# Row sums, output-weight sums and the first output chunk's sums moved from GpSimd to VectorE, in a hybrid attention and retention layer

## The chip, the cores and the metric

One core of a Trainium2 chip. The metric is device time in microseconds (us) for one execution. The engines are written as the profile writes them: PE (TensorE), DVE (VectorE), ACT (ScalarE), POOL (GpSimd), SP (SyncE, which here only issues DMAs). Each engine works through its own queue in order, and semaphores tie the queues together.

## The reference

One layer over 2048 rows of width 1024: RMSNorm, one input projection to 7168 columns, two branches (chunk-banded attention and chunkwise retention, 8 heads each), a gated merge, an output projection with the residual, and a final RMSNorm. What matters here is the end of it:

```python
branch_a = einsum('bsf,fd->bsd', o_a * silu(g_a), w_out_attn[l])      # 512 -> 1024
o_r = retention_chunkwise(qr, kr, v_r, gn_gain[l])                    # per-head group norm inside
branch_r = einsum('bsf,fd->bsd', o_r * silu(g_r), w_out_ret[l])       # 1024 -> 1024
mixed = sigmoid(m_a) * branch_a + sigmoid(m_r) * branch_r
x = x + einsum('bsd,de->bse', mixed, w_out[l])
return rms_norm(x, final_gain)
```

All of it is float32.

## The kernel before, in words

**Split products.** Each float32 operand is split in a high part (ACT casts it to the PE's rounded float32 type) and a lower part (a subtraction, on DVE or POOL), and a product of two operands is three matmuls: high by high, high by low, low by high. A product over 512 rows of depth is 4 x 3 = 12 matmuls of 128x128 by 512 columns. One step of the kernel is three matmuls; a product is four steps.

**Strassen.** The two large projections and the output projection use a seven-product scheme. For each chunk of 256 columns or rows there are quarters `b11` to `b22` of the streamed operand and four sums `t1` to `t4` of them (`sum`, three of them chained), and the resident operand `R[0]` to `R[6]` holds quarters and sums of the other side, each as high and lower parts. The seven products go into PSUM banks named `x`, `y`, `v`, `z`, `w` and are gathered on DVE into `u2`, `u3`, `c22`.

**Stages near the change.** Behind attention and retention of the second half of the rows come
- `ba0`, `ba1`: attention's output projection, 4 chunks each, plain products `ps_ba`; each result is gated on DVE (`ga`) and stored as `ta` to DRAM (`tas`);
- `br0`, `br1`: retention's output projection, 4 chunks of 8 products each, `ps_br`. The chunk's weights `raw_br` are loaded, cast by ACT (`wh_br`) and their lower parts made on DVE (`wl_br`). Two products end one group: DVE computes `gr = (gr + 1) * psum` (line 1287), POOL adds the stored `ta` to it (line 1288), and SP stores the sum to `mxs`. The loads of `gr` and `ta` use a ring of six tiles and are issued by SP, in program order with all other SP loads and stores;
- beside these, `finish_yr` makes the resident operand of `br`: SP loads `yr`, `yv`, `rb`; DVE multiplies `yr` by the gain and gate (line 1242), POOL by the row scale `rb` (line 1245), ACT casts (line 1251), DVE subtracts (line 1252). 24 such rows in this stage;
- during `br1`, `fill_wo` is called four times: it loads four quarters of the output weights (`wo`) and makes three sums of them (`ws`) on DVE and POOL, and the high and lower parts of `R[0]`, `R[1]`, `R[3]`. `place_wo` then fills `R[4]`, `R[5]`, `R[2]`, `R[6]` while the last chunk of `br1` releases them;
- `out`: eight chunks of seven products, streamed from `mxs` by ACT's queue (`raw_out`). The first chunk goes through its products in the order (0, 4, 3, 1, 2, 5, 6), so into `x`, `z`, `x`, `y`, `v`, `w`, `z`. Its sums come from POOL; the lower parts for products 2 and 5 (of `t3` and `t4`) also, all others from DVE. Each result is added to the residual rows `xr`, squared on ACT, and multiplied by the final gain `fg` on POOL.

**What sets the order.** PE and SP always run in program order. ACT, DVE and POOL do so too while `strict` is on. It is off from the end of retention until product 2 of the last `br1` chunk (in the trace around 1752 us); there a scheduler orders these three queues by its own costs. From then on the code's order holds: `later(n, fn)` puts work `n` steps ahead, and what falls due is emitted between two steps of PE. The second use of bank `x` in output chunk 0 needs `u2` (a copy by ACT, `u_out` in the trace) to have read the first.

Of the kernel before, what the change touches and what calls it, by code (L numbers as in the profile page):

```python
# [16 lines left out]
ALU = mybir.AluOpType  # L17
# [56 lines left out]
def hybrid_kernel(  # L74
# [30 lines left out]
    def r32(ap):  # L105
        return ap.bitcast(F32)
# [7 lines left out]
    def E(name, dt=F32, shape=(P, 512)):  # L114
        return epool[0].tile(list(shape), dt, tag="e", name=name)
# [33 lines left out]
    class Sometimes(Ordered):  # L149
# [3 lines left out]
    pe, act, dve, pool = Ordered(nc.tensor), Sometimes(nc.scalar), Sometimes(nc.vector), Sometimes(nc.gpsimd)  # L153
# [12 lines left out]
    R = [  # L166
        [res.tile([P, 4, B], F32R, tag=f"r{m}{n}", name=f"r{m}{n}") for n in range(2)]
        for m in range(7)
    ]
# [75 lines left out]
    def later(n, fn):  # L245

        order[0] += 1
        deferred.append((steps[0] + n, order[0], fn, free[0]))
        deferred.sort(key=lambda e: e[:2])
# [8 lines left out]
    def put(lag, dst, src):  # L258

        later(lag, lambda: dma(dst, src))  # L260
# [75 lines left out]
    class Strassen(Chunk):  # L336
# [5 lines left out]
        def sum(self, dst, one, two, ring=None):  # L342
            b = self.b
            if dst in b:
                return
            name = f"{dst}_{self.job.name}_{self.c}"
            t = wp.tile([P, 4, P], F32, tag="t", bufs=SUMS, name=name) if ring is None else \
                ring(name).rearrange("p (k c) -> p k c", k=4)
            b[dst] = self.shaped(t)
            pool.tensor_tensor(b[dst], b[one], b[two], ALU.subtract)  # L350

        def before(self):

# [16 lines left out]
        def prepare(self, n):  # L370
            self.sums(n)
            for s in SUMS_OF:
                if s[0] == PRODUCTS[n][1]:
                    self.sum(*s)
            late = pool if n in self.job.lo_pool else dve
            self.make(n, self.b[PRODUCTS[n][1]], late)

        def product(self, n):
# [855 lines left out]
    def finish_yr(h, b, m, lead, hold=0):  # L1234

        a, u, r = (E(f"{n}_{h}_{b}") for n in ("yr", "yv", "rb"))
        dma(a, orscr[h // 2][b][h % 2])
        dma(u, urscr[h][b])
        dma(r, rsscr[b // 2][8 * b + h].rearrange("(o d) -> o d", o=1).broadcast_to([P, B]))

        def gated():
            dve.scalar_tensor_tensor(a, a, gn[:, h:h + 1], u, ALU.mult, ALU.mult)

        later(lead, gated)
        later(lead + 2, lambda: pool.tensor_tensor(a, a, r, ALU.mult))
        if m is None:
            put(lead + 8, yrscr[h], a)
            return
        wh, wl = (w[:, h % 4, :] for w in R[m])
        at = max(lead + 5, hold - steps[0])  # L1250
        later(at, lambda: act.copy(wh, a))
        later(at + 2, lambda: dve.tensor_tensor(wl, a, r32(wh), ALU.subtract))
# [31 lines left out]
    def ep_br(s):  # L1284
        def epilogue(c, i, j, ps, got):
            g, ta = got
            dve.scalar_tensor_tensor(g, g, 1.0, ps, ALU.add, ALU.mult)
            pool.tensor_tensor(g, g, ta, ALU.add)
            put(7, mxscr[2 * s + i][2 * c + j], g)

        return epilogue

    wo = {}

    def fill_wo(k):

        a = {}
        for i, j in ((0, 0), (1, 0), (1, 1), (0, 1)):
            a[i, j] = E(f"wo_{i}_{j}_{k}")
            row = (4 * j + k) * P  # L1300
            dma(a[i, j], w_out[0, row:row + P, 512 * i:512 * i + 512])
        s2, s3, s4 = (E(f"ws{n}_{k}") for n in (2, 3, 4))
        wo[4, k], wo[5, k], wo[2, k], wo[6, k] = s2, s3, a[1, 1], s4

        def place(m, t, eng):
            later(1, lambda: act.copy(R[m][0][:, k, :], t))
            later(3, lambda: eng.tensor_tensor(R[m][1][:, k, :], t, r32(R[m][0][:, k, :]), ALU.subtract))

        def sums():
            dve.tensor_tensor(s3, a[1, 0], a[0, 0], ALU.subtract)  # L1310
            place(0, a[0, 0], pool)
            dve.tensor_tensor(s2, s3, a[1, 1], ALU.add)

        def rest():
            pool.tensor_tensor(s4, a[0, 1], s2, ALU.subtract)
            place(1, a[0, 1], dve)
            pool.tensor_tensor(a[1, 0], a[1, 0], a[1, 1], ALU.add)
            place(3, a[1, 0], dve)

        later(10, sums)  # L1320
        later(13, rest)

    def place_wo(m, first, every):
        for k in range(4):
            def low(k=k):
                eng = pool if k == 2 else dve
                eng.tensor_tensor(R[m][1][:, k, :], wo[m, k], r32(R[m][0][:, k, :]), ALU.subtract)

            later(first + every * k, lambda k=k: act.copy(R[m][0][:, k, :], wo[m, k]))
            later(first + every * k + 2, low)  # L1330
# [623 lines left out]
    for h in range(HEADS):  # L1954
        later(10 + 44 * h, lambda h=h: finish_yr(h, 0, None, 18))
# [12 lines left out]
    for s, (first, every, of) in enumerate((YR_0, YR_1)):  # L1968
        for n, (i, h) in enumerate((i, h) for i in range(1 - s, 2) for h in range(HEADS)):
            hold = free_at + h % 4 if s and i and h > 3 else 0  # L1970
            later(
                first + every * n // of,
                lambda s=s, i=i, h=h, hold=hold: finish_yr(h, 2 * s + i, RYR[s][i, h // 4], 8, hold),
            )
# [60 lines left out]
```

## Time and profile before

| | us |
|---|---|
| median of 3 runs | 1936.4 |
| lowest and highest run | 1934.06, 1937.48 |
| the profiled execution | 1934.51 |
| its span (first to last instruction) | 1932.7 |
| PE busy | 1877.7 (97%) |
| DVE busy | 1353.5 (70%), 2530 instructions |
| ACT busy | 931.1 (48%) |
| POOL busy | 885.1 (46%), 733 instructions |

The TensorE clock granted was 0.997 of full speed over the span. A row of the timeline gives start, duration, engine, line, operation, output and inputs, shapes, count, and in brackets how long the engine had been idle and what released it. A row of waits gives who waited, for whom, total us, times, the longest. In a group of instructions the figures are: total busy us, mean ns, idle us before them and the releasers. L143 is the line of a helper through which all operations in strict order pass, so there one goes by tiles. The merge runs from about 1495 us, `br0` from 1586, `br1` from about 1673, the output projection from 1765 to the end.

### The profile page before, as it was taken

To read this page: it belongs to the slowest core of one execution; us is meant where nothing else is said; L and a number is where in the kernel's file an instruction comes from. 1 tells how busy PE (TensorE), PEld (TensorE's weight loads), DVE (VectorE), ACT (ScalarE), POOL (GpSimd) and SP (SyncE) were. 2 spreads that over 40 slices of the span, in tenths; PEclk is the share of its full clock that TensorE was granted. 3 is DMA by queue.
4 is the path that set the end of the run, shared out by engine and by line. 5 is a ranking of instruction groups with operands and counts; after the bars stand their busy time and mean duration, and the time that the engine had idled before them with its cause. 6 is when DMAs were issued, how large, how long until landed. Compare 5 with 4: busy or idle time off the path is not lost. (4 is left out here: it accounts for less than half of the span.)

```text
span 1932.7 us, 31908 instructions
## 1 busy us (share of the span) xinstructions
PE 1877.7 (97%) x10437; PEld 1614.5 (84%) x10437; DVE 1353.5 (70%) x2530; ACT 931.1 (48%) x1931; POOL 885.1 (46%) x733
## 2 busy tenths in 40 slices
PE   7999999999999999999999999999999999998998
PEld 6899889888888887899889888888888878886886
DVE  6979788677756558879797777775555654557665
ACT  7555554666655545343333556664555221223554
POOL 0313515546546664223515444544564115547775
PEclk9999999999999999999999999999999999999999
DMA  6586876565659988675666555555998999976673
GB/s 196 165 269 204 264 262 223 182 192 171 173 158 282 272 243 286 197 252 186 206 236 216 161 162 175 161 157 161 290 269 270 323 345 328 325 262 222 208 236 132
DMA packets 325557, 435.93 MB, mean 226 GB/s; under 512 B 29880, under 2 KB 191184, under 8 KB 325392
## 3 DMA queue, kind: packets, MB, share of 16 engines
q1 hardware_dynamic: 260096, 368.35, 59.6%
q10 hardware_dynamic: 65296, 65.55, 11.1%
q8 instruction: 83, 1.36, 0.3%
q14 instruction: 82, 0.67, 0.1%
HBM read 288.14 MB, written 145.64 MB: 224 GB/s over the span
## 5 line engine op out<-in xcount | busy, mean ns | idle before, releaser
L143 POOL TENSOR_SCALAR pr<-pr,rsum 128x640 f32<-128x640 f32 (+4 forms) x128 | 96.1, 751 | 213.7 <-DVE ptl L143 104.8
L143 PE MATMUL ps_g_z<-r,wh_g 128*128 128x512 f32 x448 | 143.7, 402 | 2.7 <-DVE c_g L143 2.7
L143 PE MATMUL ps_g_x<-r,wh_g 128*128 128x512 f32 x448 | 143.2, 401 | 1.2 <-ACT u_g L143 1.1
L143 DVE CUSTOM_DVE_ANT_0 pr<-wide,bt 128x640 f32<-128x640 f32 (+4 forms) x128 | 94.3, 736 | 62.4 <-PE wide L143 55.6
L143 ACT ACTIVATE pr<-pr,mn 128x640 f32<-128x640 f32 (+4 forms) x128 | 98.0, 766 | 81.4 <-DVE mn L143 81.4
L143 DVE TENSOR_TENSOR ptl<-tp,pth 128x384 fp32r<-128x384 f32 x168 | 96.1, 573 | 41.3 <-ACT pth L143 37.4
L143 ACT CAST pth<-tp 128x384 fp32r<-128x384 f32 x168 | 84.5, 515 | 68.5 <-PE tp L143 65.6
L143 POOL TENSOR_TENSOR l_vr<-vrt,h_vr 128x512 fp32r<-128x512 f32 x32 | 47.2, 1476 | 117.0 <-ACT h_vr L143 69.3
L143 POOL TENSOR_TENSOR sl<-sm,sh 128x384 fp32r<-128x384 f32 x64 | 70.4, 1099 | 58.3 <-ACT sh L143 46.3
L143 PEld LDWEIGHTS tp<-ident,pr 128*128 128x128 f32 x560 | 71.2, 140 | 27.3 <-POOL pr L143 2.8
L143 PE MATMUL po<-pth,va 128*128 128x256 f32 x336 | 92.5, 296 | 1.2 <-DMA va<-vas 0.7
L143 POOL TENSOR_TENSOR wl_g<-t_g,wh_g 128x512 fp32r<-128x512 f32 x56 | 75.0, 1339 | 39.9 <-ACT wh_g L143 33.2
L143 PE MATMUL tp<-ident,pr 128*128 128x128 f32 x560 | 89.1, 272 | 3.0 <-POOL pr L143 1.9
L143 ACT CAST wh_p<-raw_p 128x512 fp32r<-128x512 f32 x111 | 68.0, 619 | 49.9 <-PE ps_p_y L143 15.5
L143 DVE TENSOR_TENSOR wl_p<-raw_p,wh_p 128x512 fp32r<-128x512 f32 x111 | 86.2, 783 | 7.4 <-ACT wh_p L143 6.9
L143 DVE TENSOR_TENSOR sm<-sr,dm 128x384 f32<-128x384 f32 x64 | 35.6, 556 | 78.5 <-DMA dm<-in_dmask_dram 28.2
L143 PE MATMUL wide<-ka,qa 128*128 128x384 f32 (+1 forms) x448 | 88.3, 313 | 2.2 <-DVE mn L143 2.1
L143 PEld LDWEIGHTS wide<-ka,qa 128*128 128x128 f32 x448 | 74.6, 188 | 18.6 <-DVE mn L143 8.7
L143 PE MATMUL po<-ptl,va 128*128 128x256 f32 x336 | 88.3, 284 | 1.4 <-DVE ptl L143 0.2
L143 PE MATMUL ps_g_x<-r,wl_g 128*128 128x512 f32 x224 | 88.2, 394 | 0.0
L143 PE MATMUL ps_g_z<-r,wl_g 128*128 128x512 f32 x224 | 88.1, 393 | 0.0
L143 PEld LDWEIGHTS ps_g_x<-r,wh_g 128*128 128x128 f32 x448 | 75.8, 189 | 10.7 <-ACT u_g L143 2.5
(930 smaller groups left out, 6217.3 us busy)
## 6 DMA issues: line engine op xcount, KB each, us to landing
raw_g<-in_w_in_dram ACTq DMA_DIRECT2D x56, 512.0 KB, 5.1
raw_p<-in_w_in_dram ACTq DMA_DIRECT2D x50, 512.0 KB, 5.7
qa<-qas SPq DMA_DIRECT2D x128, 128.0 KB, 3.1
qr<-qrs SPq DMA_DIRECT2D x128, 128.0 KB, 4.6
vr<-vrs SPq DMA_DIRECT2D x64, 256.0 KB, 5.4
ka<-kas SPq DMA_DIRECT2D x56, 256.0 KB, 3.2
va<-vas SPq DMA_DIRECT2D x40, 256.0 KB, 3.3
kds<-kdt_k SPq DMA_DIRECT2D x32, 256.0 KB, 3.3
```

The costliest lines, as they stand in the source:

```text
L143: return tc.keep_in_program_order(op(*a, **k))
```

## The change

Where an instruction ran on POOL, it runs on DVE: the product with `rb` in `finish_yr` (only the 24 calls in the merge, `m` not None), the row sum in `ep_br` (32), two sums and a lower part in each `fill_wo` (12), one lower part in each `place_wo` (4), and in output chunk 0 the four sums and the two lower parts that were on POOL (6; `lean()` is true there only). Nothing else moves; the later output chunks keep their sums and those lower parts on POOL.

```diff
             b[dst] = self.shaped(t)
-            pool.tensor_tensor(b[dst], b[one], b[two], ALU.subtract)
+            (dve if self.lean() else pool).tensor_tensor(b[dst], b[one], b[two], ALU.subtract)
+
+        def lean(self):
+            return self.job.name == "out" and self.c == 0
...
-            late = pool if n in self.job.lo_pool else dve
+            late = pool if n in self.job.lo_pool and not self.lean() else dve
...
-        later(lead + 2, lambda: pool.tensor_tensor(a, a, r, ALU.mult))
+        later(lead + 2, lambda: (pool if m is None else dve).tensor_tensor(a, a, r, ALU.mult))
...
             dve.scalar_tensor_tensor(g, g, 1.0, ps, ALU.add, ALU.mult)
-            pool.tensor_tensor(g, g, ta, ALU.add)
+            dve.tensor_tensor(g, g, ta, ALU.add)
             put(7, mxscr[2 * s + i][2 * c + j], g)
...
-            place(0, a[0, 0], pool)
+            place(0, a[0, 0])
...
-            pool.tensor_tensor(s4, a[0, 1], s2, ALU.subtract)
-            place(1, a[0, 1], dve)
-            pool.tensor_tensor(a[1, 0], a[1, 0], a[1, 1], ALU.add)
-            place(3, a[1, 0], dve)
+            dve.tensor_tensor(s4, a[0, 1], s2, ALU.subtract)
+            place(1, a[0, 1])
+            dve.tensor_tensor(a[1, 0], a[1, 0], a[1, 1], ALU.add)
+            place(3, a[1, 0])
...
-                eng = pool if k == 2 else dve
-                eng.tensor_tensor(R[m][1][:, k, :], wo[m, k], r32(R[m][0][:, k, :]), ALU.subtract)
+                dve.tensor_tensor(R[m][1][:, k, :], wo[m, k], r32(R[m][0][:, k, :]), ALU.subtract)
```

More of the change, by code (lines that the diff above doesn't have):

```diff
@@ L1303, in fill_wo, with place @@
         wo[4, k], wo[5, k], wo[2, k], wo[6, k] = s2, s3, a[1, 1], s4
-        def place(m, t, eng):
+        def place(m, t):
             later(1, lambda: act.copy(R[m][0][:, k, :], t))
-            later(3, lambda: eng.tensor_tensor(R[m][1][:, k, :], t, r32(R[m][0][:, k, :]), ALU.subtract))
+            later(3, lambda: dve.tensor_tensor(R[m][1][:, k, :], t, r32(R[m][0][:, k, :]), ALU.subtract))
         def sums():
             dve.tensor_tensor(s3, a[1, 0], a[0, 0], ALU.subtract)
-            place(0, a[0, 0], pool)
+            place(0, a[0, 0])
             dve.tensor_tensor(s2, s3, a[1, 1], ALU.add)
         def rest():
-            pool.tensor_tensor(s4, a[0, 1], s2, ALU.subtract)
-            place(1, a[0, 1], dve)
-            pool.tensor_tensor(a[1, 0], a[1, 0], a[1, 1], ALU.add)
-            place(3, a[1, 0], dve)
+            dve.tensor_tensor(s4, a[0, 1], s2, ALU.subtract)
+            place(1, a[0, 1])
+            dve.tensor_tensor(a[1, 0], a[1, 0], a[1, 1], ALU.add)
+            place(3, a[1, 0])
         later(10, sums)
```

## The prediction

> **What bounds the kernel now.** I began with the page: how busy each engine is and the chain that ended last.
>
> ```profile
> span 1932.7 us, 31908 instructions
> PE 1877.7 (97%) x10437; PEld 1614.5 (84%) x10437; DVE 1353.5 (70%) x2530; ACT 931.1 (48%) x1931; POOL 885.1 (46%) x733
> PE 7%; DVE 0%; ACT 0%; issue 0%; DVEq 0%
> 1787.88 3.00 PE ps_out_z L143 x12
> 1790.88 2.72 PE ps_out_x L143 x12
> ```
>
> TensorE (PE) is busy 97% of the span. The chain in order of time (the last two rows) shows 2.72 us for one product of twelve matmuls, and from 1787.88 on it runs product after product with no wait between them until the last one; the tail behind that is not touched. So the change can only win, or lose, PE's waits before that point. These are PE's waits from the merge to the second output chunk:
>
> ```profile
> PE ps_out_x L143 <- ACT u_out L143: 2.8, 1, 2.8
> PE ps_br_(0, 0)_20577 L143 <- DVE wl_br_(0, 1)_20526 L300: 2.2, 1, 2.2
> PE ps_out_y L143 <- DVE wl_out L143: 1.1, 1, 1.1
> PE ps_out_z L143 <- DVE c_out L143: 0.7, 1, 0.7
> PE ps_ba_(0, 0)_19020 L143 <- ACT wh_ba_(0, 0)_18940 L299: 0.7, 1, 0.7
> PE ps_out_w L143 <- POOL wl_out L143: 0.5, 1, 0.5
> ```
>
> Five lie between 1744 and 1788: 2.2 in the last chunk of `br1`, then 2.8, 1.1, 0.5 and 0.7 in output chunk 0, together 7.3 us. That is the pot. The `ba` wait (0.7) hangs on a late weight load, which is not edited. Next I read the vector queues around the two large waits.
>
> ```profile
> 1743.13 1.29 POOL L1307 TENSOR_TENSOR r<-wo,r 128x512 fp32r<-128x512 f32 x1 [11.34 <-ACT r L1306]
> 1744.38 1.71 POOL L1288 TENSOR_TENSOR gr<-gr,ta 128x512 f32<-128x512 f32 x1
> 1743.17 1.80 DVE L1310 TENSOR_TENSOR ws<-wo,wo 128x512 f32<-128x512 f32 x1 [2.78 <-DMA wo<-in_w_out_dram]
> 1744.89 1.74 DVE L300 TENSOR_TENSOR wl_br_(0, 1)_20526<-raw_br,wh_br_(0, 1)_20525 128x512 fp32r<-128x512 f32 x1
> 1746.56 1.77 DVE L1312 TENSOR_TENSOR ws<-ws,wo 128x512 f32<-128x512 f32 x1
> 1750.78 0.67 DVE L1287 SCALAR_TENSOR_TENSOR gr<-gr,ps_br_(1, 0)_20493 128x512 f32<-128x512 f32 x1
> 1771.96 0.68 DVE L143 SCALAR_TENSOR_TENSOR gr<-gr,ps_br_(1, 1)_20702 128x512 f32<-128x512 f32 x1
> 1772.56 0.68 DVE L143 TENSOR_TENSOR wl_out<-raw_out,wh_out 128x512 fp32r<-128x512 f32 x1
> 1773.16 1.76 DVE L143 TENSOR_TENSOR r<-wo,r 128x512 fp32r<-128x512 f32 x1
> ```
>
> The same 128x512 subtraction on VectorE (DVE) takes 0.68 us with starts 0.60 us apart when GpSimd (POOL) is idle (1772.56), and 1.74 to 1.80 when POOL runs beside it (1743.17, 1744.89, 1773.16). POOL needs 1.29 alone and 1.71 contended. The product with a PSUM operand is 0.67 to 0.68 either way. So a pair side by side costs each engine about 1.75 us for what DVE alone does in 0.60 each. The Trainium skill (SBUF — State Buffer, section Who interferes with whom) says that a VectorE instruction with two SBUF inputs and a GpSimd instruction that reads SBUF exclude each other for a whole instruction; 0.68 against 1.74 agrees.
>
> The 2.2 us wait is this: `wl_br_(0, 1)` was queued behind the weight difference at 1743.17, and both were stretched. The 2.8 us wait comes by a longer way, through SyncE (SP) and ScalarE (ACT):
>
> ```profile
> SPq L143 <- POOL gr L1288: 8.5, 2, 4.6
> 1746.11 0.32 SPq L143 DMA_DIRECT2D mxs<-gr  x1
> 1753.23 0.32 SPq L143 DMA_DIRECT2D mxs<-gr  x1
> 1756.58 0.32 SPq L143 DMA_DIRECT2D ta<-tas  x1
> 1759.68 1.29 POOL L143 TENSOR_TENSOR gr<-gr,ta 128x512 f32<-128x512 f32 x1 [2.29 <-DMA ta<-tas]
> 1763.95 0.32 SPq L143 DMA_DIRECT2D ta<-tas  x1
> 1764.80 0.42 SPq L143 DMA_DIRECT2D xr<-in_x_dram  x1
> 1769.10 0.37 ACTq L143 DMA_DIRECT2D raw_out<-mxs  x1
> 1769.56 0.62 ACT L143 CAST wh_out<-raw_out 128x512 fp32r<-128x512 f32 x1 [3.63 <-DMA xr<-in_x_dram]
> 1773.21 0.57 ACT L143 COPY u_out<-ps_out_x 128x512 f32<-128x512 f32 x1
> ```
>
> SP issues in order and stood up to 4.6 us for one row sum `gr += ta` on POOL (1753.23). Each later `ta` load comes 3.35 us behind the store of a row sum whose buffer it takes (1753.23 to 1756.58; it landed 3.1 us on, when the sum at 1759.68 began), and the stores queue behind it, so a late sum makes the whole row of `ta`, store, `ta`, store late, up to the `xr` load at 1764.80. By the profile ACT's load of `raw_out` (1769.10) was released by that `xr` landing, and seven casts behind the one at 1769.56 stands `u_out`, which ends at 1773.8 (1773.21 + 0.57) and for which PE waits. So what starts the row is a sum on POOL, and each link behind it is a store and a load.
>
> **The change part by part.** 78 instructions go from POOL to DVE: 24 products `yr`, 32 sums `gr += ta`, 12 in `fill_wo`, 4 in `place_wo`, 4 sums and 2 lower parts of output chunk 0. The groups:
>
> ```profile
> L1288 POOL TENSOR_TENSOR gr<-gr,ta 128x512 f32<-128x512 f32 x29 | 44.4, 1538 | 55.7 <-DVE gr L1287 34.6 <-issue 11.4 <-DMA rb<-rss 4.2
> L1245 POOL TENSOR_TENSOR yr<-yr,rb 128x512 f32<-128x512 f32 x24 | 31.7, 1320 | 77.4 <-DVE yr L1242 35.8 <-DMA ga<-mas 24.4 <-DMA rb<-rss 17.3
> L1252 DVE TENSOR_TENSOR r<-yr,r 128x512 fp32r<-128x512 f32 x24 | 17.9, 745 | 57.2 <-ACT r L1251 57.2
> L1310 DVE TENSOR_TENSOR ws<-wo,wo 128x512 f32<-128x512 f32 x4 | 5.7, 1434 | 17.5 <-DMA wo<-in_w_out_dram 17.5
> L143 POOL TENSOR_TENSOR gr<-gr,ta 128x512 f32<-128x512 f32 x3 | 4.7, 1562 | 4.7 <-DMA ta<-tas 2.3 <-DVE gr L143 1.2 <-DVE r L143 1.2
> 1580.00:1740.00 160.00, 160.00 (x707) 132.49 (x706) 81.56 (x106) 32.00 (x55) 73.81 (x51) 1.00 0.90 308
> 1740.00:1790.00 50.00, 42.69 (x183) 33.77 (x182) 38.82 (x39) 19.07 (x37) 38.09 (x25) 1.00 0.66 219
> ```
>
> (The last two rows are busy time by stretch: its length, then PE, PEld, DVE, ACT and POOL. PE's 42.69 of 50.00 is the pot again.) DVE takes 78 x 0.60 = 47 us, POOL gives up some 110 (78 x about 1.4).
>
> *The 24 `yr` products.* DVE now idles 57.2 us over the 24 lower parts, 2.4 each, waiting for ACT behind POOL's 1.32. With the product on DVE (0.60) that chain is shorter by about 0.7, and the product fills idle time. New risk: DVE itself now waits for `rb`. POOL's three waits for it total 17.3 us, but mostly count POOL's idleness before DVE was ready. Bounds: no cost, to DVE held for a few us. PE is busy all 160.00 us from 1580 to 1740, although DVE stood most of its 17.5 us of waits for `wo` in there; waits of a few us are covered. I take 0.
>
> *The 32 row sums.* 0.60 each on DVE, directly behind the product that feeds them. What is queued behind a sum that waits for `ta`: lower parts and PSUM evacuations. In the trace one sum of 32 waited for `ta` (2.3 in the row of three; the row of 29 names none), and that one because the store two rows above it was late. With the product at 1750.78 followed at once by its sum, the store goes out at 1752.1 at the latest, not 1753.23.
>
> *Output weights (16).* In `fill_wo` a row of four weights costs DVE 7 instructions in place of 4. In the last row: the difference at 1743.17 takes 0.60, `wl_br_(0, 1)` the next 0.60, so it ends at 1744.4; PE, which waited 2.2 us until 1746.6 (1744.89 + 1.74), wants it at 1744.4. If the scheduler puts the newly moved lower part ahead, 0.6 us of the wait stays. Gain of this wait by itself 1.6 to 2.2. Then come two sums, the difference, two lower parts and the product of 1750.78: 8 instructions by 0.60 behind 1743.17, and about 0.7 for the casts, put it at 1748.7, its sum at 1749.3, the store at 1750.0: 3.2 us earlier. The sum at 1744.38 no longer waits behind a lower part (its store was at 1746.11), so SP is freed some 3 to 4 us earlier too, and loads ahead of it move up: I take the SP row as 3.2 to 5.5 earlier, 4.4 in the middle.
>
> *Output chunk 0 (6).* Here the order is the written one. Count DVE's queue from the end of PE's last product but two of `br1` (half 1, column 0 of the last chunk): first that half's `gr` product, its sum, and then lower parts of weights, two sums of the chunk and so on; the last `gr` product is the 14th, its sum the 15th, the lower part for the next product into `ps_out_x` the 16th, for `ps_out_y` the 20th, for `ps_out_v` the 24th. At 0.60 they are there after 9.6, 12.0 and 14.4 us. PE wants them after 4, 5 and 6 products of 2.72: 10.9, 13.6 and 16.3. So DVE leads by 1.3 to 1.9 us where it is 1.1 late now, and the waits of 1.1, 0.5 and 0.7 go. What is late next is POOL's neighbourhood: it keeps chunk 1's sums, and two of them fall here. Each can stretch a DVE neighbour by 1.1 (0.68 to 1.76): 2.2 against a lead of 1.6, so I charge 0.6, between 0 and, with four such meetings, 2.5. By the rule of the section cited above alone, every remaining POOL instruction blocks one of DVE's, the 2.5 hold, and the sum below would be 4.2; no row shows how many really meet.
>
> *The sum.* The first wait and the 2.8 us do not add freely: PE at `ps_out_x` is ready at 1771.0 (1773.8 less 2.8) and 2.2 earlier without the first wait, but `u_out` ends only as much earlier as the SP row moves. PE's shift there is the smaller of 2.2 + 2.8 = 5.0 and 4.4, so 4.4. Then 1.1 + 0.5 + 0.7 = 2.3, less 0.6: 6.1 us. If the SP row moves by 3.2 it is 4.9, with four meetings 4.2; if all waits go, 7.3. The profiled execution took 1934.5 (span 1932.7 and 1.8 around it), 1.9 below the median of 1936.4, so 1928.4 beside it and 1930.3 for the median.
>
> **The rivals.**
> *A. The SP row stays where it is.* The scheduler orders the stretch before 1751 by its own costs and could leave the product of 1750.78 late, or SP may be held by landings, not sums: in that stretch it also waited for those.
>
> ```profile
> SPq L143 <- DMA mxs<-gr: 9.5, 5, 2.5
> ```
>
> Then `u_out` ends at 1773.8 as before, the first gain is eaten there, and only 2.3 us of the later waits go: 1934.1. Against it: the longest single hold was a sum.
>
> *B. Slower: DVE held by `ta`.* DVE takes its queue in order: it stood 9.1 us for one cast while evacuations behind it were ready.
>
> ```profile
> 1739.10 0.69 DVE L300 TENSOR_TENSOR wl_br_(0, 0)_20507<-raw_br,wh_br_(0, 0)_20506 128x512 fp32r<-128x512 f32 x1 [9.11 <-ACT wh_br_(0, 0)_20506 L299]
> ```
>
> The Trainium skill (TensorE: Matmul & The Clock Gate, section Architectural detail, where it gives queue depths) also calls the vector queue a strict FIFO. The place is the last sum: DVE gets there at the earliest when PE ends (1765.5, two products ahead of the 1771.0 above), by the count 3.0 us later, 1768.5. The `ta` issued at 1763.95 lands 3.1 later, 1767.1, without any gain on SP. It decides once `ta` lands over 1.3 us (the lead) behind DVE; to end 4 us slower with the pot unwon, that far again, or some four sums must hold DVE by 2.3 each beyond the lead. Time then: about 5 us above the median, 1941. Against it: one such wait in 32, and SP's row moves ahead, not back.
>
> *C. No change.* The moved work reaches DVE in an order that makes other lower parts late by as much as is won (DVE is busy 70% overall): new waits of about 6 us in the same 45 us, 1936.
>
> **How the numbers follow.** Forecast (4.2 to 7.3 us won, 1929.1 to 1932.2) 0.58; A 0.20; C 0.13; B 0.09. What a measurement of this kernel can tell from no change is 0.2%, 3.9 us: the forecast lies beyond it, A and C within, with a tenth of A beyond (0.02 more), and B beyond on the other side. So faster 0.61, same 0.30, slower 0.09. The range: at the low end all 7.3 us and the `ba` wait of 0.7 give 1928.4, and the runs before reach 2.3 below their median (1934.06), of which I allow 1.4: 1927.0. At the high end it takes in A and nearly all of C, 1936.5, and leaves out B.
>
> **What would show it.** Right: the row of PE's waits between 1740 and 1790 loses `wl_br_(0, 1)` and the output lower parts; the DVE subtractions there have 0.68, not 1.7; the store of 1753.23 is 3 us or more ahead; `u_out` comes within half a us of its product's end. Wrong: a wait of PE on `u_out` of the old size (A), a DVE wait for `ta` or `rb` of several us followed by PE waits (B), new PE waits between 1500 and 1740, or an unchanged span with POOL merely emptied (C).

## The result, and the profile after

The changed kernel took 1927.43 us (median of five runs, 1925.94 to 1928.17), the kernel before, run beside it, 1935.7: a ratio of 0.9956 with a 95% interval of 0.9942 to 0.9969. The profiled execution took 1925.94 us against 1934.51, its span 1923.9 against 1932.7.

The head of the page of the changed kernel:

```profile
span 1923.9 us, 31855 instructions
PE 1876.7 (98%) x10437; PEld 1615.8 (84%) x10437; DVE 1379.8 (72%) x2608; ACT 931.4 (48%) x1931; POOL 770.8 (40%) x655
```

DVE has exactly 78 instructions more and POOL 78 fewer; DVE is 26 us busier and POOL 114 less busy. PE does the same work in a span that is 8.8 us shorter. All of PE's waits from 1500 to 1800 us, and the busy time by stretch (length, then PE, PEld, DVE, ACT and POOL, then the granted clock):

```profile
PE ps_ba_(0, 0)_19212 L143 <- ACT wh_ba_(0, 0)_19136 L299: 1.4, 1, 1.4
```

```profile
1580.00:1740.00 160.00, 160.00 (x707) 132.50 (x706) 108.47 (x169) 36.19 (x60) 0.00 (x0) 1.00 0.92 317
1740.00:1790.00 50.00, 50.00 (x222) 41.39 (x222) 37.48 (x58) 21.10 (x42) 16.81 (x10) 1.00 0.61 202
```

The five waits are all gone: PE is busy for 50.00 of the 50 us from 1740 to 1790, where it had 42.69. To place the gain, I take one stage, from the first product of `br0` to the last of the output projection. Its first and last rows in PE's timeline, first of the kernel before, then of the changed one:

```profile
1588.82 0.62 PE L143 MATMUL ps_br_(0, 0)_19295<-r,wh_br_(0, 0)_19229 128*128 128x512 f32 x2
...
1924.04 0.28 PE L143 MATMUL ps_out_end<-r,wl_out 128*128 128x256 f32 x1
```

```profile
1589.08 0.39 PE L143 MATMUL ps_br_(0, 0)_19295<-r,wh_br_(0, 0)_19229 128*128 128x512 f32 x1
...
1915.51 0.28 PE L143 MATMUL ps_out_end<-r,wl_out 128*128 128x256 f32 x1
```

From start to start the stage takes 335.22 us before and 326.43 after: 8.79 less, the whole difference of the spans. Below, "stage" is this time; it is free of what happens ahead of 1588, which alone differs by up to 10 us between kernels whose code there is nearly the same.

The timeline of the changed kernel where the waits were:

```profile
1731.32 0.69 DVE L300 TENSOR_TENSOR wl_br_(0, 1)_20526<-raw_br,wh_br_(0, 1)_20525 128x512 fp32r<-128x512 f32 x1
...
1734.76 0.69 DVE L1313 TENSOR_TENSOR ws<-wo,wo 128x512 f32<-128x512 f32 x1 [2.15 <-DMA wo<-in_w_out_dram]
...
1739.58 0.69 DVE L1291 TENSOR_TENSOR gr<-gr,ta 128x512 f32<-128x512 f32 x1
1740.29 0.32 SPq L143 DMA_DIRECT2D mxs<-gr  x1
...
1754.29 0.42 SPq L143 DMA_DIRECT2D xr<-in_x_dram  x1
...
1761.22 0.40 ACTq L143 DMA_DIRECT2D raw_out<-mxs  x1
...
1766.08 0.59 ACT L143 COPY u_out<-ps_out_x 128x512 f32<-128x512 f32 x1 [0.62 <-PE ps_out_x L143]
...
1770.55 4.04 POOL L143 TENSOR_TENSOR t_out<-raw_out 128x512 f32<-128x512 f32 x1 [263.21 <-DVE wl_out L143]
```

The weight difference that took 1.80 (at 1743.17) takes 0.69. The store that stood at 1753.23 goes out at 1740.29, the `xr` load of 1764.80 at 1754.29, and `u_out` follows its product instead of holding the next one. The lower part `wl_br_(0, 1)`, for which PE had waited 2.2 us, now stands ahead of that weight difference in DVE's queue (first row); before, it stood behind it. The last row is a new thing: POOL's first sum of output chunk 1 takes 4.04 us while DVE works back to back beside it.

### The profile page after: what moved, and what is told of

Same layout as the page of the kernel before. It is cut to its first block, busy times and chain, and to the rows that moved or that the text cites. A ratio compares the mean times of both kernels' runs of the same rounds, so it can differ in the third digit from the quotient of the medians.

```text
span 1923.9 us, 31855 instructions
## 1 busy us (share of the span) xinstructions
PE 1876.7 (98%) x10437; PEld 1615.8 (84%) x10437; DVE 1379.8 (72%) x2608; ACT 931.4 (48%) x1931; POOL 770.8 (40%) x655
## 4 chain that ended last, share of the span: by engine, by line
PE 53%; DVE 4%; DMA 4%; issue 1%; SPq 1%; ACT 1%; POOL 0%; DVEq 0%; POOLq 0%; ACTq 0%
PE ps_p_x L143 4%; PE ps_g_z L143 4%; PE ps_p_z L143 4%; PE ps_g_x L143 4%; PE po L143 2%; PE ps_out_z L143 2%; PE ps_out_x L143 2%; PE ps_g_v L143 2%; PE ps_g_y L143 2%; PE wide L143 2%; PE ps_p_y L143 2%; PE ps_p_v L143 2%; PE ps_p_w L143 2%; PE ps_g_w L143 2%; PE o L143 2%
## 5 line engine op out<-in xcount | busy, mean ns | idle before, releaser
L143 POOL TENSOR_TENSOR t_out<-raw_out 128x512 f32<-128x512 f32 x7 | 14.1, 2009 | 263.2 <-DVE wl_out L143 263.2
```

The costliest lines, as they stand in the source:

```text
L143: return tc.keep_in_program_order(op(*a, **k))
```

## The experiments

Two theories can explain the gain. The *lock theory*: a POOL instruction that reads SBUF beside a DVE instruction with two SBUF inputs stretches both, and that makes lower parts late. The *path theory*: the row sums on POOL come late, hold SP's queue, and so hold ACT and `u_out`. The prediction had both in its sum. Each ratio below is against the kernel before on the same chip; waits and stage come from one profile of each kernel.

| kernel | ratio, 95% interval | stage, us | PE's waits, 1700 to 1800 |
|---|---|---|---|
| before | | 335.22 | 2.2, 2.8, 1.1, 0.5, 0.7 |
| before, second profile | 1.0003 [0.9987, 1.0019] | 333.67 | 0.8, 2.2, 1.3, 0.5, 0.7 |
| changed | 0.9956 [0.9942, 0.9969] | 326.43 | none |
| row sums only (32) | 0.9969 [0.9954, 0.9984] | 327.56 | 0.7 |
| all but row sums (46) | 0.9957 [0.9943, 0.9972] | 327.32 | 0.2 |
| weights only (16) | 0.9980 [0.9967, 0.9993] | 330.08 | 1.3, 1.7 |
| weights and chunk 0 (22) | 0.9973 [0.9961, 0.9985] | 327.34 | 0.2 |
| chunk 0 only (6) | 0.9998 [0.9984, 1.0012] | 331.79 | 0.5, 2.8, 0.5, 0.2 |
| `yr` only (24) | 1.0002 [0.9988, 1.0015] | 332.75 | 2.3, 0.5, 0.7 |
| changed, reading ghosts (78) | 1.0014 [1.0000, 1.0027] | 334.49 | 1.7, 2.6, 1.3 |
| changed, writing ghosts (78) | 0.9967 [0.9956, 0.9977] | 326.43 | none |
| changed, late stores | 0.9971 [0.9961, 0.9981] | 326.43 | none |
| changed, reading ghosts in chunk 0 | 0.9978 [0.9965, 0.9990] | 327.35 | 0.6 |
| changed, reading ghosts in the merge | 1.0012 [0.9997, 1.0027] | 331.64 | 0.8, 1.7, 0.5, 0.5 |

### Which part is needed

The row sums alone (line 1291 of the changed kernel; the rest as before):

```diff
-            pool.tensor_tensor(g, g, ta, ALU.add)
+            dve.tensor_tensor(g, g, ta, ALU.add)
```

> Only the 32 row sums go to VectorE; the other 46 instructions stay on GpSimd. Path theory (late sums on GpSimd hold SyncE's queue, and through it the loads): the store that left at 1753.2 us leaves 8 us or more earlier, the waits on wl_br_(0, 1) and on u_out go, those of 1.1, 0.5 and 0.7 stay; 5 to 6 us won, ratio about 0.997. Lock theory (the two engines stretch each other's 0.7 and 1.3 us to 1.75): more than half of the GpSimd work still lies beside VectorE's, most waits stay, at most 3 us won, ratio 0.9985 or more.

The reverse, everything but the row sums:

```diff
-            dve.tensor_tensor(g, g, ta, ALU.add)
+            pool.tensor_tensor(g, g, ta, ALU.add)
```

> As the changed kernel, but the 32 row sums are back on GpSimd, alone there. Path theory, strict form (the sums themselves must leave GpSimd): the stores stay late, the wait on u_out of 2.8 us returns, at most 5 us won, ratio about 0.9975. Queue form (the sums were late only because weights' work stood before them on GpSimd): each sum starts within 0.1 us of its product, stores are at most 2 us later than in the changed kernel, 7 us or more won, ratio 0.9965 or less. Lock theory: 32 of 78 meetings remain, some 3 us of waits come back, ratio about 0.997.

All of PE's waits from 1700 to 1800 in the one and in the other:

```profile
PE ps_out_z L143 <- DVE c_out L143: 0.7, 1, 0.7
```

```profile
PE ps_out_z L143 <- DVE c_out L143: 0.2, 1, 0.2
```

Either half takes nearly all waits away. The parts do not add: the stage is 7.7 us shorter with the row sums alone and 7.9 with everything else, and 8.8 with both. So the row sums need not leave POOL, and the reading that they alone hold SP's row up is false: with all else moved, most sums start within 0.1 us of their product, as the queue form had it, and the 3 us of waits that the lock theory expected back do not come.

The lock theory also fails on the row sums alone: it expected most waits to stay and 0.9985 or more. The path theory's 0.997 came, and the two large waits went; the 1.1 and 0.5 that it left standing went as well, and why those two went is not shown. Yet the weights' pairs still stretch DVE there. Two rows of DVE with the row sums alone:

```profile
1741.60 0.69 DVE L300 TENSOR_TENSOR wl_br_(0, 1)_20526<-raw_br,wh_br_(0, 1)_20525 128x512 fp32r<-128x512 f32 x1 [0.59 <-ACT wh_br_(0, 1)_20525 L299]
...
1744.25 1.80 DVE L1310 TENSOR_TENSOR ws<-wo,wo 128x512 f32<-128x512 f32 x1 [1.35 <-DMA wo<-in_w_out_dram]
```

Here too the scheduler has put `wl_br_(0, 1)` ahead of the weight difference, out of reach of the stretched pair. This order is a second way to lose the 2.2 us wait, but not a needed one: with all but the row sums, and with the weights alone (below), that lower part still stands behind the difference (at 0.69 us), and PE does not wait for it.

Output chunk 0's six instructions alone (`lean()` as in the change, all else as before):

```diff
+        def lean(self):
+            return self.job.name == "out" and self.c == 0
```

> Only the four sums and two lower parts of output chunk 0 go to VectorE. Path theory: the store at 1753.2 us and the waits of 2.2 and 2.8 us stay; the wait on GpSimd's lower part (0.5) goes, the one of 1.1 us shrinks; 0.5 to 2 us won, ratio 0.999 to 1.000. Lock theory: six meetings fewer in the stretch where VectorE is fullest, the waits of 1.1, 0.5 and 0.7 go, and u_out's shrinks; 3 us won, ratio about 0.9985.

The `u_out` wait keeps its 2.8 us and the ratio is 0.9998: the path theory's case; the 3 us that the lock theory expected did not come. (The wait on `wl_br_(0, 1)` is 0.5, against 2.2 and 0.8 in the two profiles of the kernel before.) The other side of that split, only the 16 in `fill_wo` and `place_wo`:

```diff
-            pool.tensor_tensor(s4, a[0, 1], s2, ALU.subtract)
+            dve.tensor_tensor(s4, a[0, 1], s2, ALU.subtract)
...
```

> Only the 16 instructions of fill_wo and place_wo go to DVE; row sums, yr products and the first output chunk's sums stay on POOL. Lock theory (a POOL instruction beside a DVE one stretches both, and that is what makes PE wait): the pairs around 1743 go, so the waits of 2.2 and 2.8 us go; some of the three later waits (1.1, 0.5, 0.7) stay: 4 to 6 us won, ratio about 0.997 to 0.998. Rival (the gain needs several parts together): at most 3 us, ratio 0.9985 or above.

All of PE's waits from 1700 to 1800 with the weights alone:

```profile
PE ps_out_z L143 <- DVE c_out L143: 1.7, 1, 1.7
PE ps_out_y L143 <- DVE wl_out L143: 1.3, 1, 1.3
```

As the lock theory had it: the waits of 2.2 and 2.8 go, while waits inside chunk 0 stay, where POOL still makes the chunk's sums (1.3 and 1.7, for 1.1, 0.5 and 0.7); 0.998, and a stage 3.6 to 5.1 us shorter. Both together, 22 of the 78 instructions:

> The 22 instructions of the weights and of output chunk 0 go to DVE; the 24 yr products and the 32 row sums stay on POOL. Lock theory, with the place of the neighbour as what counts: nearly all of the gain, 6 to 8.5 us, ratio 0.997 or below, no wait of PE above 0.5 between 1700 and 1790. Rival (row sums and yr products count): 4 us or less, ratio 0.998 or above, with the waits for u_out or wl_br still there.

One wait of 0.2 is left, the stage is 327.34 and the ratio 0.9973: the lock theory's case in waits and stage, with a ratio just above its 0.997; the interval overlaps that of the full change. And the 24 `yr` products alone:

```diff
-        later(lead + 2, lambda: pool.tensor_tensor(a, a, r, ALU.mult))
+        later(lead + 2, lambda: (pool if m is None else dve).tensor_tensor(a, a, r, ALU.mult))
```

> Only the 24 yr products go to DVE. They lie between 1531 and 1683 us, 60 us ahead of PE's first large wait. Lock theory: nothing to win there, 0 to 1 us, ratio 0.9995 to 1.000, all five waits of PE (2.2, 2.8, 1.1, 0.5, 0.7) still there within 1 us in sum. Rival (the yr products were what kept POOL's row sums late): the waits of 2.2 and 2.8 shrink by 2 us or more together, ratio 0.999 or below.

1.0002, as expected in time. The waits were 3.5 us in sum, not within 1 us of 7.3: those on `wl_br_(0, 1)` and on chunk 0's second lower part are missing. The second profile of the kernel before, below, has 5.5, so a part of this is how much the kernel before varies. The rival's sign came in part, for 2.2 and 2.8 became 0 and 2.3, but not in the ratio; against the second profile's 0.8 and 2.2 it is 0.7 less. The shorter waits did not shorten the stage as much: PE's stretch around the 2.3 us wait was granted 0.93, which by estimate costs some 1.8 us (0.07 of 25).

```profile
1765.00:1790.00 25.00, 21.53 (x85) 16.37 (x85) 23.91 (x23) 10.97 (x24) 20.93 (x14) 0.93 0.66 232
```

### Is it the reading beside DVE?

The changed kernel, with a "ghost" on POOL behind each of the 78 instructions: a sum of 480 columns of its result into a scratch tile that nobody reads.

```diff
+    def ghost(src):
+        gh = ghs[0]
+        src = src[:, 0:480] if len(src.shape) == 2 else src[:, :, 0:120]
+        pool.tensor_tensor(gh if len(src.shape) == 2 else gh.rearrange("p (k c) -> p k c", k=4), src, src, ALU.add)
```

> As the changed kernel, but behind each of the 78 moved instructions GpSimd adds the result (or, for lower parts, the high part or the summed operand) to itself into a scratch tile of 480 columns that nobody reads: GpSimd is as busy as before the change, but nobody waits for it. Path theory: VectorE's instructions are stretched, yet stores and loads stay early; within 2 us of the changed kernel, ratio to before 0.9955 to 0.9966. Lock theory: VectorE has 78 instructions more and the old stretching; the waits of 1.1, 0.5, 0.7 us return larger and new ones come; 5 us or more of the 8 lost, ratio 0.998 or more.

And its control, a ghost that takes POOL's time at the same places but reads one column instead of 960:

```diff
+        pool.tensor_copy(gh[:, 0:1], one)
+        pool.memset(gh, 0.0)
+        pool.memset(gh, 0.0)
```

> The changed kernel, and behind each of the 78 moved instructions POOL copies one column of its result and fills a scratch tile of 480 columns with zeros twice: POOL has work at the same places as in the run with added reading sums, but reads one column instead of 960. If two engines exclude each other only when both read SBUF: as the changed kernel within 2 us, ratio 0.997 or below, DVE subtractions at 0.69. If any work of POOL beside DVE costs: as with the reading sums, ratio 0.999 to 1.002, DVE subtractions at 1.2 or more beside it.

Reading ghosts: all of PE's waits from 1700 to 1800, the stretch from 1740 to 1790, and one group of DVE's lower parts in that stretch:

```profile
PE ps_out_y L143 <- DVE wl_out L143: 2.6, 1, 2.6
PE ps_out_x L143 <- DVE wl_out L143: 1.7, 1, 1.7
PE ps_out_z L143 <- DVE wl_out L143: 1.3, 1, 1.3
```

```profile
1740.00:1790.00 50.00, 44.46 (x186) 35.64 (x185) 46.30 (x54) 17.01 (x32) 30.58 (x23) 0.97 0.62 205
```

```profile
L143 DVE TENSOR_TENSOR r<-ws,r 128x512 fp32r<-128x512 f32 x12 | 12.8, 1101 | 0.0
```

Writing ghosts, the last two (PE had no wait from 1700 to 1800):

```profile
1740.00:1790.00 50.00, 50.00 (x222) 41.39 (x222) 38.69 (x58) 20.30 (x41) 37.52 (x65) 1.00 0.65 208
```

```profile
L143 DVE TENSOR_TENSOR r<-ws,r 128x512 fp32r<-128x512 f32 x12 | 7.8, 684 | 0.0
```

POOL is busier with the writing ghosts (37.52 us of 50) than with the reading ones (30.58), yet DVE's lower parts keep 684 ns against 1101, and the gain stays whole (0.9967) where the reading ghosts eat it (1.0014). Not POOL's load but its reading beside DVE is the price. The section of the Trainium skill that the prediction cites (SBUF — State Buffer, Who interferes with whom) says the same of a GpSimd instruction that only writes: it does not contend with such a DVE instruction. The two runs agree with it.

Two limits. The old waits on `wl_br_(0, 1)` and `u_out` did not come back with the reading ghosts; the new ones, 5.6 us, are all on lower parts of the output. So the ghosts show what reading beside DVE costs, and that the weights' pairs made the waits of 2.2 and 2.8 rests on the run with the weights alone. And not all of the 8.1 us by which the reading ghosts lengthen the stage is waiting: the clock granted from 1765 to 1790 was 0.93, again some 1.8 us by estimate.

Is it the neighbours inside chunk 0, or those ahead of it? Reading ghosts only behind chunk 0's six instructions, and only behind the row sums and the weights (the same `ghost`, its other calls left out):

> The changed kernel with the added reading sums on POOL behind the 6 instructions of output chunk 0 alone. If it is the neighbours in chunk 0, where DVE leads PE by less than 2 us, that cost: waits of PE for output lower parts of 2 us or more in sum, half of what all 78 cost, ratio 0.9985 or above. If it is the crowd ahead of it that makes DVE's queue late: at most 2 us lost, ratio 0.997 or below.

> The changed kernel with the added reading sums on POOL behind the 32 row sums and the 16 instructions of the weights, none in output chunk 0 and none behind the yr products. If the neighbours in chunk 0 are what costs: at most 2 us lost, ratio 0.997 or below. If it is the crowd ahead of it, of which about 15 instructions fall due together with the chunk: PE waits for output lower parts of 2 us or more in sum, ratio 0.9985 or above.

The 48 ghosts of the merge cost 5.2 us of stage, the 6 of chunk 0 cost 0.9. So the neighbours inside the chunk are not the whole, as the second expectation had it. But that the place counts is not shown: per ghost the two cost about the same (0.11 and 0.15 us), and about 15 of the 48 fall due together with the chunk. PE's waits are all on `wl_out`, in chunk 0, in both; there DVE is only just ahead of PE (by 0.6 to 1.2 us in the changed kernel, below), so a delay brought along from ahead of the chunk would show up there too. The ratio of the first (0.9978) lies between the two bounds that were set, so its 0.9 us rests on the stage.

### Is the SP row a cause?

The changed kernel, with each row sum handed to SP later by POOL work that hardly reads:

```diff
+    def late_g(g):
+        gh = ghs[0]
+        pool.tensor_copy(gh[:, 0:1], g[:, 0:1])
+        for _ in range(6):
+            pool.memset(gh, 0.0)
+        pool.tensor_copy(g[:, 0:1], g[:, 0:1])
...
             dve.tensor_tensor(g, g, ta, ALU.add)
+            late_g(g)
```

> The changed kernel, and behind each of the 32 row sums POOL copies one column of it, fills a scratch tile of 480 columns with zeros six times (about 0.56 us each) and copies that column onto itself; the store to mxs waits for it, so every row sum reaches SP some 4 us later, while POOL hardly reads SBUF. Path theory (a late row of ta, store, ta, store on SP holds the load in front of u_out): the xr load behind the stores moves 4 us or more, PE waits 2 us or more for u_out, half of the gain or more is lost, ratio 0.998 or above. Contention theory alone (only reading work of POOL beside DVE costs): DVE at 0.69, no wait for u_out, within 2 us of the changed kernel, ratio 0.9968 or below.

The last store ahead of the `xr` load, that load, ACT's load behind it, and `u_out`:

```profile
1759.67 0.32 SPq L143 DMA_DIRECT2D mxs<-gr  x1
1760.04 0.42 SPq L143 DMA_DIRECT2D xr<-in_x_dram  x1
...
1763.19 0.37 ACTq L143 DMA_DIRECT2D raw_out<-mxs  x1
...
1767.69 0.59 ACT L143 COPY u_out<-ps_out_x 128x512 f32<-128x512 f32 x1 [0.28 <-issue]
```

The `xr` load comes 4.2 us later in the stage than in the changed kernel, and PE does not wait: the path theory, as expected there, fails. The ratio, 0.9971, lies between the bounds of the two theories (0.9968 and 0.998). (Only the last three sums were held the full 4 us; in the stretch that the scheduler orders, it put the closing copy ahead of five of the six fills.) But this does not clear the row. Here is every kernel's first `xr` load and the start of `u_out`, both counted from the first `br0` product:

| kernel | `xr` load | `u_out` starts | PE's wait for `u_out` |
|---|---|---|---|
| changed | 165.2 | 177.0 | none |
| the eight others without that wait | 165.2 to 167.8 | 177.0 to 178.3 | none |
| late stores | 169.4 | 177.0 | none |
| `yr` only | 173.4 | 181.6 | 2.3 |
| chunk 0 only | 173.8 | 182.7 | 2.8 |
| before, second profile | 174.4 | 182.6 | 2.2 |
| before | 176.0 | 184.4 | 2.8 |

Where the load comes at 173.4 or later, `u_out` starts 8.2 to 8.9 us behind it, four times of four; up to 169.4 it starts at 177.0 to 178.3, and PE does not wait for it. In these four kernels, and in none of the other ten, the profile names the `xr` load as what released ACT's last cast of `raw_out` ahead of `u_out` (before: 1769.56). So the row is the path of the 2.8 us wait, and in the changed kernel it has over 4 us to spare. This is read from the traces: no run makes the row alone late by the 8 us that it would take. The row is late where the weights' pairs and the row sums both sit on POOL, and early as soon as one of them leaves.

### The kernel before once more

The kernel before, unedited, for a second profile:

> The kernel before once more, unedited, for a second profile of it. In one profile its stretch from the first product of the merge's second part to the last output product takes 335.2 us against 326.4 in the changed kernel (8.8 less), while the medians of eight edited kernels lie on average some 2 us nearer to before than their stretches do. If the first profile is typical: 334.7 to 335.7 us again and the same five waits of PE (2.2, 2.8, 1.1, 0.5, 0.7 within 0.4 each). If it was a slow one: 332 to 334, one of the waits gone or smaller by 1 us or more. Ratio 1.000 within its interval.

The first profile has the longer stage: it is 333.67 now, with the same five waits, but 5.5 us in sum and not 7.3; the wait on `wl_br_(0, 1)` was 0.8 in place of 2.2. So the change is worth 7.2 us in the stage by this execution and 8.8 by the first. In the median the worth is less certain than one interval says: the writing ghosts and the late stores have the changed kernel's stage to the hundredth, but their medians are only 5.8 and 5.4 us below the kernel before, against its 8.3. Nothing that I ran beats the changed kernel; moving all but the row sums has the same ratio and a stage 0.9 us longer.

## Why the prediction was right, point by point

The forecast was a gain of 6.1 us; the stage gave 7.2 to 8.8 and the medians 8.3. The time, 1927.43, lies below the forecast's own 1929.1 to 1932.2 and 0.4 above the low end of the range. That end held by some luck: it had 1.4 us for scatter and 0.7 for a `ba` wait, of which nothing came (1.3 us of `ba` waits before, 1.4 after), and 0.7 of the distance to 1930.3 is only that the median of the kernel before is now 1935.7 and not 1936.4. The direction, the stretch of the trace and the engines at work held. Three terms were off in size, and one part of the cause. (A slip beside: the chances of faster, 0.58 and 0.02, make 0.60 and not 0.61.)

**The pot was too small.** I took it as 7.3 us of waits. The prediction's own chain has a product right behind a wait at 3.00 us (1787.88) and one in full flow at 2.72. Each of the five waits thus costs 0.28 more: 7.3 + 5 x 0.28 = 8.7, against the stage's 8.79. Read from start to start in PE's timeline, the products around the waits are longer by 2.51, 3.12, 1.39 and, for the last two waits together, 1.76: 8.78. In the second profile it is 5.5 + 1.4 = 6.9 against 7.24. The low end of the range was built on the same 7.3.

**The SP row was sized from its last link only.** I had it 3.2 to 5.5 us earlier, and so let it cap the first two waits at 4.4. The store is 12.9 earlier and the `xr` load 10.5 (10.8 within the stage). I counted from the weight difference at 1743.17, but the row ahead of it was late in the same way: in the kernel before, a row sum on POOL (1728.93) stood behind three weight instructions, yet POOL was idle for 1.89 us ahead of it. What it waited for last was its product on DVE (1728.12, ended at 1728.80), whose matmuls had ended at 1719.5, and which stood behind the weights' lower parts there. Behind the sum stood SP's store, the `raw_br` loads and the next four `wo` loads. DVE's, POOL's and SP's timeline of before, then SP's after:

```profile
1726.02 2.17 DVE L1307 TENSOR_TENSOR r<-wo,r 128x512 fp32r<-128x512 f32 x2
1728.12 0.68 DVE L1287 SCALAR_TENSOR_TENSOR gr<-gr,ps_br_(1, 1)_20363 128x512 f32<-128x512 f32 x1
...
1725.30 1.75 POOL L1315 TENSOR_TENSOR ws<-wo,ws 128x512 f32<-128x512 f32 x1
1728.93 2.86 POOL L1288 TENSOR_TENSOR gr<-gr,ta 128x512 f32<-128x512 f32 x2 [1.89 <-issue]
...
1730.57 0.32 SPq L143 DMA_DIRECT2D mxs<-gr  x1
...
1735.30 4.87 SPq L143 DMA_DIRECT2D wo<-in_w_out_dram  x4
```

```profile
1723.79 0.32 SPq L143 DMA_DIRECT2D mxs<-gr  x1
...
1727.08 3.48 SPq L143 DMA_DIRECT2D wo<-in_w_out_dram  x4
```

That store is 6.8 us earlier, the next `wo` loads 8.2: the delay had been passed on from one call of `fill_wo` to the next. With the row out of the way the two waits give their full 5.0, and the spare of over 4 us shows that the row had more than it needed.

**The charge of 0.6 for POOL's sums in output chunk 1 did not fall due, and the cover was thinner than counted.** The lower parts for `ps_out_x`, `ps_out_y` and `ps_out_v` end 0.6, 0.9 and 1.2 us ahead of PE in the changed kernel, where I had 1.3, 1.6 and 1.9. Half of the difference is that I counted 0.60 from start to start throughout, while three starts in this row lie 0.72 apart, such as the last row sum behind the product that it reads (1766.00 to 1766.72).

```profile
1767.33 0.69 DVE L143 TENSOR_TENSOR wl_out<-raw_out,wh_out 128x512 fp32r<-128x512 f32 x1
...
1769.74 0.68 DVE L143 TENSOR_TENSOR wl_out<-t_out,wh_out 128x512 fp32r<-128x512 f32 x1
...
1772.14 0.69 DVE L143 TENSOR_TENSOR wl_out<-t_out,wh_out 128x512 fp32r<-128x512 f32 x1
```

```profile
1768.60 0.62 PE L143 MATMUL ps_out_x<-r,wh_out 128*128 128x512 f32 x2
...
1771.32 0.62 PE L143 MATMUL ps_out_y<-r,wh_out 128*128 128x512 f32 x2
...
1774.04 0.62 PE L143 MATMUL ps_out_v<-r,wh_out 128*128 128x512 f32 x2
```

POOL's sum of 1770.55 lies right beside them, and took the delay itself: 4.04 us, while DVE stayed at 0.68 to 0.69 per instruction until 1773.9. The 4.2 us won that the prediction gave for the rule of the Trainium skill alone (four such meetings) did not come: one meeting fell before PE's need, and it went against POOL. That was luck as far as the runs show. The same sum at the same place, with all but the row sums moved, cost DVE 1.1 us:

```profile
1769.09 1.62 POOL L143 TENSOR_TENSOR t_out<-raw_out 128x512 f32<-128x512 f32 x1 [2.49 <-issue]
1769.49 2.38 DVE L143 TENSOR_TENSOR r<-ws,r 128x512 fp32r<-128x512 f32 x2
```

With the weights and chunk 0 it did the same (1.62 and 2.38), and both kernels keep a wait of 0.2. The ghosts in chunk 0, with a wait of 0.6, also show that a meeting there can cost.

**The `yr` products at nothing: right.** Their cover is there: DVE's idle time in front of the 24 lower parts falls from 57.2 to 14.1, and `rb` holds DVE for 2.8 in all. The rows of DVE's groups after, from 1495 to 1790 (total busy, mean ns, idle before):

```profile
L1291 DVE TENSOR_TENSOR gr<-gr,ta 128x512 f32<-128x512 f32 x29 | 19.9, 687 | 0.3
L1255 DVE TENSOR_TENSOR r<-yr,r 128x512 fp32r<-128x512 f32 x24 | 16.6, 692 | 14.1 <-ACT r L1254 13.8
L1248 DVE TENSOR_TENSOR yr<-yr,rb 128x512 f32<-128x512 f32 x24 | 16.6, 691 | 3.3 <-DMA rb<-rss 2.8
L143 DVE TENSOR_TENSOR gr<-gr,ta 128x512 f32<-128x512 f32 x3 | 2.1, 692 | 0.1
```

**The rivals.** A (the row stays) is out: the row moved by over 10 us. B (DVE held by `ta`) is out by the first and last of these rows: 0.4 us of idle time before 32 sums. C (new waits as large as the old) is out: there are none; but it is what the reading ghosts made, 5.6 us of new waits on output lower parts, so it was a real way to lose. The prediction's picture of the cause, POOL's sums as the start of the row, was half of it: the sums were late because the weights' instructions stood ahead of them on POOL (the sum of 1744.38) or ahead of their products on DVE (1728.12 and 1750.78), and moving either the weights' instructions or the sums off POOL is enough.

## What to carry to other kernels

Read who stretches whom before counting busy shares: two engines at 70% and 46% held PE up for over 7 us, because their instructions met, and stood in each other's way, at one place. When several waits hang on one cause, do not add the parts of a change; look for the smallest part that is enough (here 22 of the 78 instructions take away all but 0.2 us of wait, and the 32 row sums all but 0.7). Follow a late queue back over more than one turn of its loop before sizing what it gains.

## What the runs showed of the hardware that was not expected

- How a pair is shared is not fixed. POOL's 128x512 subtraction takes 1.29 us alone (1759.68 before) and about 1.75 in most meetings. Beside an unbroken row of DVE instructions the same one took 4.04 us and DVE lost nothing until the end of it (changed kernel; 4.03 with the reading ghosts in chunk 0), or 1.62 and DVE lost 1.1 (all but row sums). What decides it stays open.
- POOL's fills of 480 columns, 38 of them by 0.50 us from 1740 to 1790, left DVE's lower parts at 684 ns (686 in the changed kernel).
- A wait of PE costs about 0.28 us more than its length: the product behind it takes 3.00 us in place of 2.72. In two of the runs the granted clock also fell around the waits (0.93 over 25 us with `yr` only, 0.97 over 50 us with all reading ghosts), while it was 1.00 over those 50 us in the kernel before, with 7.3 us of idle time there; why in these two stays open.
- The stretches ahead of the edit differ by up to 10 us from kernel to kernel with nearly the same code there (PE reaches `br0` between 1586.1 and 1595.9), so a change of this size is read more safely from its own stage than from one total.
